# Layer 0's long-convolution filters moved ahead of the first conditioning block

## The chip, the cores and the metric

The kernel runs on one core of one Trainium2 chip, as one program. The metric is device time in microseconds (us) of one launch; lower is better. Three runs of the kernel before took 1815.71, 1817.62 and 1821.91 us, median 1817.62 us.

## The reference, cut to what matters

A two-layer network over 256 context and 256 latent tokens of 2048 features. In each layer a conditioning vector c is turned into a shift and a scale per feature by a matrix `ada_w` of 2048 x 6144; the normalised tokens, scaled and shifted, go through one wide projection `w_in` (2048 x 6688) whose columns feed four mixers. One of them (Hyena) convolves with filters of length 256 that a small network generates from the positions alone, so they depend on no token and no conditioning.

```python
for i in range(DEPTH):
    mod_l = jax.nn.silu(c) @ ada_w[i] + ada_b[i]
    mod_c = jax.nn.silu(c_ctx) @ ada_w[i] + ada_b[i]
    sh_l, sc_l, gt_l = jnp.split(mod_l[:, None, :], 3, axis=-1)
    ...
    h_l = _rmsnorm(x_l, norm_w[i]) * (1.0 + sc_l) + sh_l
    h_c = _rmsnorm(x_c, norm_w[i]) * (1.0 + sc_c) + sh_c
    pl = _project(h_l, w_in[i], SEG_NAMES)
    ...
    hy_l = _hyena_seq(pl['hy_x'], hy_conv_w[i], hy_conv_b[i], hy_filt, hy_bias[i])

def _hyena_filters(L, w1, b1, f1, w2, b2, f2, w3, b3, f3, w4):
    ...
    h = jnp.sin(f1 * (z @ w1 + b1))
    h = jnp.sin(f2 * (h @ w2 + b2))
    h = jnp.sin(f3 * (h @ w3 + b3))
    h = (h @ w4).reshape(L, 2, HY_ORDER, BR)
    ...
    return k * lax.rsqrt(jnp.sum(k * k, axis=0, keepdims=True) + EPS)
```

## The kernel before

Everything is float32. A weight w is split on the chip into two parts, `whi` (a cast on ScalarE, line 922) and `wlo` (w minus `whi`, on VectorE or GpSimd, line 180); the tokens likewise (tile `hs`). A projection is then three TensorE products per block: whi times high part, whi times low part, wlo times high part.

`run` (line 1407) starts a launch: it loads the 512 tokens in 16 tiles (line 1419), sums squares, makes `rrow` (one over the rms along the tokens, two lines from `junk` tiles, and a copy to a tile `mA`), and transposes the tokens into `xT`. Then `layer0_qk` computes the first eight projection units of 256 columns. It goes over the 2048 features in five stages, because a feature block can be projected only when its conditioning is known: `STAGES = (0, 1, 2, 4, 6, 8)`, so stages 0 and 1 hold 256 features each and stages 2 to 4 hold 512 each. For every stage:

- `ada` loads the stage's columns of `ada_w` in blocks of 256 KB through SyncE's queue into `raw` tiles (line 1037) and multiplies them on TensorE (psum tile `pa`, line 195): 16 loads for stage 0, 16 for stage 1, 32 for each later one. After the last block the sums are copied on ScalarE (`adr`), transposed on TensorE (`pa<-c_kc,adr`), and added to the bias (`mod`).
- `make_h` scales and shifts the feature blocks: `tr` on VectorE, `hs` high on ScalarE (line 1199), `hs` low on VectorE. It needs `mod` and `rrow`.
- every unit loads its 256 KB of `w_in` (line 934) and makes 12 products of 512 columns into psum tiles `pj` and `pB`. `steps` takes loads of the next stage's `ada` in between.

768 such products make up `layer0_qk`; stages 0 and 1 hold 96 each. The S5 mixer of layer 0 starts when they are done.

`hy_kf(0, ...)` (line 480) generates the filters. It is a Python generator, so nothing of it is issued until it is advanced. Its first part issues seven loads on SyncE's queue (four of `hy_w4`, line 486; two of `hydec`, line 489; one of `kdft`, line 491) and calls `hy_filters`: small loads on GpSimd's queue, one transposition to `hyv`, and three layers, each a TensorE product into psum tile `pA`, seven short VectorE instructions and a sine on ScalarE (line 476). The second part makes, for each of two orders, nine products of 128x512 into `pA` with VectorE multiplications, squares on ScalarE, additions on GpSimd, and four stores to DRAM (`kfd`, lines 531 and 532) on SyncE's queue. In `run` the whole generator was advanced inside `between(1)`, after stage 1's `make_h`; it is followed there by `s5_params(0)`.

The instructions' order on each engine isn't the order of the code. A scheduler simulates the program with its own costs, starts from the code's order as priority, takes what is ready, and allots buffers: two psum banks `pA`, two `pB`, three `pj`, nine `raw` tiles, 18 tiles each of `mA` and `mB`. The order that it writes is fixed: on the chip each engine goes through its own list in that order, and so does each queue of loads.

Of the kernel before, what the change touches and what calls it, by code (L numbers as in the profile page):

```python
# [15 lines left out]
PSUM = bass.MemoryType.PSUM  # L16
DRAM = bass.MemoryType.DRAM
# [5 lines left out]
T = 512  # L23
# [92 lines left out]
class Net:  # L116
# [36 lines left out]
    def const2(self, ap):  # L153
        """a constant of 512 columns or fewer, loaded where it is used"""
        t = self.t2()
        n = 1
        for d in ap.shape[1:]:
            n *= d
        v = t[:ap.shape[0], :n]
        if len(ap.shape) > 2:  # L160
            ap = ap.rearrange("p a b -> p (a b)")
        self.nc.scalar.dma_start(v, ap)
        return v
# [46 lines left out]
    def exp_acc(self, out, x, n, r, ni):  # L210
        """exp to float32 accuracy on small tiles: 2^n * poly(x - n ln 2); ni: int32 scratch"""
        nc = self.nc
        nc.vector.tensor_scalar(out, x, -104.0, 89.0, op0=OP.max, op1=OP.min)
        x = out
        nc.vector.tensor_scalar(n, x, 1.0 / math.log(2.0), MAGIC, op0=OP.mult, op1=OP.add)
        nc.vector.tensor_scalar(n, n, MAGIC, -127.0, op0=OP.subtract, op1=OP.max)
        nc.vector.tensor_scalar(n, n, 128.0, None, op0=OP.min)
        self.stt(r, n, -L1, x)
        self.stt(r, n, -L2, r)
        nc.vector.tensor_scalar(out, r, 1.0 / 5040, None, op0=OP.mult)  # L220
        for k in (720, 120, 24, 6, 2, 1):
            self.stt(out, out, 1.0 / k, r, op0=OP.add, op1=OP.mult)
        nc.vector.tensor_scalar(n, n, 127.0, None, op0=OP.add)
        self.cp(ni, n, 'v')
        nc.vector.tensor_scalar(ni, ni, 23, None, op0=OP.logical_shift_left)
        self.stt(out, out, 1.0, ni.bitcast(F32), op0=OP.add, op1=OP.mult)

    def rsqrt_mean(self, r, ss, n, c0=0, g=1):
        """r = 1/sqrt(ss/n + eps) on a small tile, on columns c0.. of each of g groups"""
        r, ss = (x.rearrange("p (g c) -> p g c", g=g)[:, :, c0:] for x in (r, ss))  # L230
        self.nc.scalar.activation(r, ss, AF.Sqrt, bias=self.eps[:r.shape[0]], scale=1.0 / n)
        self.nc.vector.reciprocal(r, r)

# [20 lines left out]
    def gla(self, i, v, qd, kd_, vd, lrs, lat_only, y_cb):  # L254
        """qd (x 1/8), kd_: [256, 512] and vd: [512 tok, 512] in DRAM; lrs: 4 tiles [128 tok, 32]"""
# [12 lines left out]
        t = self.t2()  # L268
# [5 lines left out]
        for ct in range(2):  # L274
# [9 lines left out]
            for d in range(2):  # L284
# [18 lines left out]
                kd = self.t2()  # L303
# [79 lines left out]
    def norm_out(self, o, r, lo, h, y_cb):  # L383
        """o: token tiles [128 tok, 128] of one head, r: their 1/rms -> y [128 dv, tokens]"""
        p = self.pm()
        for n, x in enumerate(o):
            self.nc.vector.tensor_scalar(x, x, r[:, n:n + 1], None, op0=OP.mult)
            self.tr(p[:, lo + n * 128:lo + (n + 1) * 128], x)
        y_cb(h, p)

# [1 line left out]
    def ret(self, qd, kd, vd, lat_only, y_cb):  # L392
        """qd, kd: [512, 512] and vd: [512 tok, 512] in DRAM"""
# [55 lines left out]
    def hy_filters(self, i):  # L449
        """the last hidden layer of the filter network, [64, 256 positions], twice on the partitions"""  # L450
# [28 lines left out]
    def hy_kf(self, i, kfd):  # L479
        """KF[order][parity][re/im] as tiles [128 m, 512 ch]; yields once its inputs are under way and after each order"""  # L480
# [54 lines left out]
    def hy_conv(self, v, ct, p, lat_only):  # L535
        """short conv of one tile of 128 channels from PSUM"""
# [11 lines left out]
    def hyena(self, i, v, kfd, xd, lat_only, y_cb):  # L548
        """xd: [1536, segs x 256] in DRAM"""
# [72 lines left out]
    def cmul(self, orr, oi, ar, ai, br, bi, t1, t2, eng=('v', 'v')):  # L622
        """(orr, oi) = (ar + i ai)(br + i bi)"""
# [8 lines left out]
    def s5_params(self, i):  # L632
        """per-layer arrays, (direction, state) on partitions and groups on the free axis"""
# [101 lines left out]
    def s5_gen(self, i, P, hb):  # L735
        """matrices of groups 4hb..4hb+3"""
# [71 lines left out]
    def s5_run(self, u, G, lat_only, y):  # L808
        """u: [(t, i), 4 groups x 64 chunks] -> y [(t, o), 4 groups x chunks]"""
# [50 lines left out]
    def s5_store_u(self, ud):  # L860
        """[128 ch, 512 tok] -> DRAM [group, (i, 7 - t), chunk], token = 8 chunk + t"""
# [69 lines left out]
    def wpart(self, src, r0, c0, w, step=True, keep=False):  # L931
        """rows r0..r0+255, columns c0..c0+w-1 of a weight matrix as hi and lo, [128, 2, w]; keep: in tiles of their own"""
# [21 lines left out]
    def proj_part(self, W, kq, c0, ps, t0, first, last, step=True):  # L954
        """rows 256 kq.. of (h @ W[:, c0:c0+256])^T into the two banks ps"""
# [10 lines left out]
    def proj_t(self, W, c0, ncol, t0, cb, step=True):  # L966
        """(h @ W[:, c0:c0+ncol])^T for tokens t0.., in tiles of 128 columns: cb(j, psum[:, tokens])"""
# [8 lines left out]
    def proj_n(self, W, c0, w, toks, cb, banks=None, order=range(8), step=True, keep=False):  # L976
        """x @ W[:, c0:c0+w] with tokens on partitions: cb(tt, psum[:, :w]); keep: one token tile after the other"""
# [44 lines left out]
    def ada(self, i, cols, n, group, done):  # L1022
        """n columns of the modulation from each of the two in cols, as four pieces of n / 2: row 32j + v of the
        result is piece j of stream v (0 latent, 1 context). Yields after every load; the products come after every
        group-th, as a change between them and full-width ones costs the tensor engine a drain."""
# [26 lines left out]
    def ada_cols(self, r, adab, k0, m):  # L1052
        """m[128, (sh, sc), k, v] for feature blocks k0.. from the four pieces (sh, sc) x 2 in r"""
# [10 lines left out]
    def ada_feat(self, i, f0, n, m, adab, group=GRP):  # L1064
        """the modulation of features f0..f0+n-1"""
        return self.ada(i, (f0, 2048 + f0), n, group, lambda r: self.ada_cols(r, adab, f0 // 128, m))

    def ada_el(self, i, cols, nv, done, eng):
        """ada for 512 columns from each of the two in cols and the first nv streams, with the products off the
        tensor engine, which only sums over the partitions"""  # L1070
# [66 lines left out]
    def gate_row(self, i, v, j):  # L1137
        """512 columns of the gate of stream v on every partition"""
# [22 lines left out]
    def rstd(self, ss):  # L1161
        """ss [128, token tiles, pieces] -> 1/rms [128, token tiles]"""
# [7 lines left out]
    def rrow(self, rs):  # L1170
        """[128, 512]: 1/rms of the 4 x 128 tokens along the columns, on every partition"""
# [9 lines left out]
    def warm_sqrt(self, ss):  # L1181
        """brings the square root's table in before it is waited for"""
# [3 lines left out]
    def make_h(self, k, x, m, vec, rrow):  # L1186
        """hi and lo of block k of h^T from x^T [128, 512]; rrow: 1/rms along the tokens"""
# [52 lines left out]
    def qk_units(self, lat):  # L1240
        """the projections of s5_u and of the q and k of GLA and retention: (name, width, first token, callback)"""
# [7 lines left out]
    def layer0_qk(self, xT, m, adab, vec, rrow, between):  # L1249
        """the projections of qk_units in layer 0, over the feature quarters as their modulation becomes known"""  # L1250
# [141 lines left out]
    def w_out(self, i, c, toks, t0, x, gt, ss, step=True, done=None):  # L1392
        """column piece c (256 wide) of x += gate * (y @ w_out); sums of squares of the rows"""
# [13 lines left out]
    def run(self, out):  # L1407
# [15 lines left out]
        hk = self.hy_kf(0, kfd[0])  # L1423
        ss = self.sm.tile([128, 4, 8], F32, name="xss")
# [13 lines left out]
        self.hh, self.hl = [], []  # L1438
        Ps = {}

        def between(f):
            self.cur = 'A'
            if f == 1:
                for _ in hk:
                    pass
# [140 lines left out]
```

## Time and profile before

| | us |
|---|---|
| median of three runs (lowest to highest) | 1817.62 (1815.71 to 1821.91) |
| profiled execution: span from first to last instruction | 1809.3 |
| TensorE busy | 1714.9 (95%) |
| VectorE busy | 1283.9 (71%) |
| ScalarE busy | 753.5 (42%) |
| GpSimd busy | 552.2 (31%) |

The profile gives the span of the profiled execution and no other time of it; the median run is 8.3 us longer than that span (launch and end lie outside it), and this distance is taken as it is. PE is TensorE's matmuls and PEld its weight loads; DVE, ACT, POOL and SP are VectorE, ScalarE, GpSimd and SyncE, and a name with q is the engine's issuing side, where loads are issued. One matmul of float32 data by this program shows as several records, and neighbouring records overlap by about a tenth of a us, since their ends are modelled. A load is listed where it is issued, with the time that the issue took.

### The profile page before, as it was taken

What the parts mean: (1) busy time and instruction counts of PE and PEld (TensorE: products, weight loads), DVE (VectorE), ACT (ScalarE), POOL (GpSimd) and SP (SyncE); (2) the same over time, 40 slices, a digit from 0 to 9 for tenths busy, and PEclk for the clock granted to TensorE, in tenths of its full rate; (3) what the DMA queues carried; (4) which work ended last, traced back from release to release, by engine and by line L of the source; (5) the groups of instructions that cost most, each with busy time, mean ns of one, the idle gap of its engine ahead of it and who ended that gap; (6) DMA issues with size and microseconds to landing.
All of it is one profiled execution on the core that took longest, in us unless ns stands there. A gap on an engine that the chain in (4) does not pass through costs nothing. (4 is left out here: it accounts for less than half of the span.)

```text
span 1809.3 us, 33542 instructions
## 1 busy us (share of the span) xinstructions
PE 1714.9 (95%) x12320; PEld 1412.7 (78%) x12320; DVE 1283.9 (71%) x2393; ACT 753.5 (42%) x1462; POOL 552.2 (31%) x524
## 2 busy tenths in 40 slices
PE   7999999998999999999999999698999899999997
PEld 4656678877766668876788899477987788999997
DVE  2477774669997666965888584777768776668754
ACT  5333252244344434232334434555354545454544
POOL 4024022223323100101144734468434231121353
PEclk9999999999999999999999999799999999999999
DMA  9868755556464678668866555466453336788963
GB/s 295 258 233 234 248 169 165 167 172 202 126 182 152 194 220 266 197 204 267 290 213 213 173 154 182 121 184 205 140 164 108 105 91 196 239 262 256 283 202 123
DMA packets 308029, 355.18 MB, mean 196 GB/s; under 512 B 42433, under 2 KB 227481, under 8 KB 307865
## 3 DMA queue, kind: packets, MB, share of 16 engines
q1 hardware_dynamic: 299936, 341.81, 61.1%
q10 hardware_dynamic: 5112, 8.79, 1.6%
q0 software_dynamic: 2816, 2.43, 0.9%
q8 instruction: 97, 1.59, 0.4%
q14 instruction: 68, 0.55, 0.1%
HBM read 316.11 MB, written 36.83 MB: 195 GB/s over the span
## 5 line engine op out<-in xcount | busy, mean ns | idle before, releaser
L195 PE MATMUL pj<-hs,whi 128*128 128x512 f32 (+1 forms) x2560 | 692.2, 356 | 12.8 <-ACT hs L1199 6.9
L922 ACT CAST whi<-raw 128x512 fp32r<-128x512 f32 (+1 forms) x536 | 329.6, 619 | 608.8 <-DMA raw<-in_w_in_dram 271.9
L180 DVE TENSOR_TENSOR wlo<-raw,whi 128x512 fp32r<-128x512 f32 (+1 forms) x428 | 334.1, 786 | 275.1 <-ACT whi L922 263.7
L195 PEld LDWEIGHTS pj<-hs,whi 128*128 128x128 f32 x2560 | 443.3, 190 | 104.2 <-issue 27.4
L994 PE MATMUL pj<-whi,hs 128*128 128x256 f32 (+1 forms) x2368 | 455.0, 289 | 5.8 <-ACT tr L1377 2.3
L195 PE MATMUL pj<-hs,wlo 128*128 128x512 f32 (+1 forms) x1280 | 451.2, 354 | 1.1 <-DVE wlo L180 1.0
L180 POOL TENSOR_TENSOR wlo<-raw,whi 128x512 fp32r<-128x512 f32 (+1 forms) x108 | 159.4, 1476 | 793.5 <-ACT whi L922 680.6
L994 PEld LDWEIGHTS pj<-whi,hs 128*128 128x128 f32 x2368 | 374.0, 191 | 24.0 <-issue 15.4
L994 PE MATMUL pj<-wlo,hs 128*128 128x256 f32 (+1 forms) x1184 | 340.8, 288 | 0.0
L195 PEld LDWEIGHTS pj<-hs,wlo 128*128 128x128 f32 x1280 | 241.9, 189 | 38.6 <-issue 6.5
L180 POOL TENSOR_TENSOR mA<-mA 128x512 f32<-128x512 f32 x120 | 173.9, 1462 | 226.5 <-ACT mA L511 84.7
L994 PEld LDWEIGHTS pj<-wlo,hs 128*128 128x128 f32 x1184 | 226.0, 191 | 4.3 <-issue 3.8
L195 PE MATMUL pA<-mA 128*64 128x64 f32 (+6 forms) x1276 | 160.6, 307 | 25.9 <-DVE mA L180 19.5
L180 DVE TENSOR_TENSOR mA<-mA 128x512 f32<-128x512 f32 (+6 forms) x246 | 155.0, 658 | 22.3 <-DMA mA<-rq 17.8
L192 DVE SCALAR_TENSOR_TENSOR acc<-raw,sc,acc 128x512 f32<-128x512 f32 x180 | 142.1, 819 | 8.4 <-DMA raw<-in_ada_w_dram 8.2
L195 PEld LDWEIGHTS pA<-mA 128*64 128x64 f32 (+3 forms) x1276 | 102.8, 151 | 57.6 <-issue 16.7
L195 PE MATMUL pB<-mB 64*64 64x128 f32 (+4 forms) x896 | 101.8, 293 | 6.7 <-DVE mB L180 4.3
L180 POOL TENSOR_TENSOR acc<-acc,raw 128x512 f32<-128x512 f32 x60 | 88.6, 1477 | 63.1 <-ACT raw L1086 52.6
L180 DVE TENSOR_TENSOR mB<-mB 128x512 f32<-128x512 f32 (+2 forms) x164 | 84.1, 546 | 14.1 <-ACT mB L292 8.3
L195 PEld LDWEIGHTS pB<-mB 64*64 64x64 f32 (+2 forms) x896 | 66.0, 152 | 30.1 <-issue 13.5
L173 ACT COPY mA<-pA 128x512 f32<-128x512 f32 (+3 forms) x118 | 45.2, 409 | 97.0 <-PE pA L195 70.0
L195 PE MATMUL pa<-raw,sc 128*32 128x256 f32 (+1 forms) x1024 | 79.7, 360 | 3.5 <-DMA raw<-in_ada_w_dram 2.3
(230 smaller groups left out, 1779.7 us busy)
## 6 DMA issues: line engine op xcount, KB each, us to landing
raw<-in_ada_w_dram SPq DMA_DIRECT2D x384, 256.0 KB, 3.9
raw<-in_w_in_dram SPq DMA_DIRECT2D x384, 256.0 KB, 3.4
raw<-in_w_out_dram SPq DMA_DIRECT2D x128, 256.0 KB, 3.3
raw<-in_w_in_dram SPq DMA_DIRECT2D x32, 272.0 KB, 3.1
mB<-kfd SPq DMA_DIRECT2D x24, 256.0 KB, 4.3
mB<-in_ctx_dram SPq DMA_DIRECT2D x16, 256.0 KB, 5.6
mB<-in_x_dram SPq DMA_DIRECT2D x16, 256.0 KB, 5.9
kfd<-mA SPq DMA_DIRECT2D x16, 256.0 KB, 4.3
```

The costliest lines, as they stand in the source:

```text
L173: self.nc.scalar.copy(out, in_)
L180: (self.nc.vector if eng == 'v' else self.nc.gpsimd).tensor_tensor(out, a, b, op=op)
L192: self.nc.vector.scalar_tensor_tensor(out, in0, scalar, in1, op0=op0, op1=op1)
L195: self.nc.tensor.matmul(out, lhsT, rhs, start=start, stop=stop)
L922: self.nc.scalar.copy(hi, x)
L994: mm = lambda a, b, start, stop: self.nc.tensor.matmul(o, a, b, start=start, stop=stop, skip_group_check=per > 1)
```

## The change

The generator is advanced once right after it is made, ahead of the sums of squares and of `rrow`, so that the seven loads and the filter network come there in the code; the rest of it runs after the token transpositions and ahead of `layer0_qk`. `between(1)` no longer advances it.

```diff
         hk = self.hy_kf(0, kfd[0])
+        next(hk)
         ss = self.sm.tile([128, 4, 8], F32, name="xss")
...
         self.hh, self.hl = [], []
+        self.cur = 'A'
+        for _ in hk:
+            pass
         Ps = {}
 
         def between(f):
             self.cur = 'A'
-            if f == 1:
-                for _ in hk:
-                    pass
             if f == 1:
                 Ps[0] = self.s5_params(0)
```

The other lines of the diff remove comments. What the scheduler made of it is seen in three places.

**SyncE's queue of loads, from the last token tiles on.** `in_x` and `in_ctx` are the tokens, `in_ada_w` the conditioning's blocks (256 KB each), `in_w_in` the projection's weights. Before:

```order
L1419 DMA mB<-in_x_dram 128x512 x2
L1037 DMA raw<-in_ada_w_dram 128x2x256 x16
L934 DMA raw<-in_w_in_dram 128x2x256
L486 DMA mA<-in_hy_w_dram 64x512
L1037 DMA raw<-in_ada_w_dram 128x2x256 x3
L934 DMA raw<-in_w_in_dram 128x2x256
L486 DMA mA<-in_hy_w_dram 64x512
L1037 DMA raw<-in_ada_w_dram 128x2x256 x2
```

With the change:

```order
L1419 DMA mB<-in_x_dram 128x512 x2
L486 DMA mA<-in_hy_w_dram 64x512 x4
L489 DMA mA<-const_hydec_dram 128x512 x2
L491 DMA mA<-const_kdft_dram 128x512
L1037 DMA raw<-in_ada_w_dram 128x2x256 x16
L934 DMA raw<-in_w_in_dram 128x2x256
L1037 DMA raw<-in_ada_w_dram 128x2x256 x3
L934 DMA raw<-in_w_in_dram 128x2x256
L1037 DMA raw<-in_ada_w_dram 128x2x256 x3
```

The filters' seven loads now stand ahead of stage 0's 16 blocks. After those 16, stage 1's 16 blocks stand in the next 22 loads, with six of `w_in` between.

**TensorE, around the first projection product (`pj<-hs,whi`).** `pa<-raw,sc` are the conditioning's products, four for each block; `pA<-mA` here the filter network's layers; `pA<-junk` the products of `rrow`; `pa<-c_kc,adr` the transposition that ends a stage's conditioning. Before:

```order
L195 MATMUL pA<-junk,c_kc 128x128
L195 MATMUL pa<-raw,sc 32x128 x36
L199 MATMUL pa<-c_kc,adr 128x128
L195 MATMUL pa<-raw,sc 32x128 x12
L195 MATMUL pj<-hs,whi 128x512 x3
```

With the change (the row ahead of these is the transposition that ends stage 0):

```order
L195 MATMUL pA<-mA 64x256
L195 MATMUL pa<-raw,sc 32x128 x24
L195 MATMUL pA<-mA 64x256
L195 MATMUL pa<-raw,sc 32x128 x24
L195 MATMUL pA<-mA 128x256
L195 MATMUL pA<-junk,c_kc 128x128 x2
L195 MATMUL pa<-raw,sc 32x128 x8
L195 MATMUL pA<-junk,c_kc 128x128
L195 MATMUL pa<-raw,sc 32x128 x4
L195 MATMUL pA<-junk,c_kc 128x128
L195 MATMUL pa<-raw,sc 32x128 x4
L199 MATMUL pa<-c_kc,adr 128x128
```

The first product of the projections, which stood behind three blocks of stage 1, now follows this list: behind the three filter layers, the four products of `rrow` and all 64 products (16 blocks) of stage 1. After five projection products come the first eight products of stage 2, which need four of its blocks. The 18 products of 128x512 that make the filters still stand between projection products, now between the 19th and the 172nd instead of the 172nd and the 321st.

**ScalarE, up to the first scaled tokens (`hs<-tr,mod`, line 1199).** `adr<-pa` ends a stage's conditioning, L476 is the filter network's sine, `mA<-pA` the copy of `rrow`. Before:

```order
L173 COPY mA<-pA 128x512
L173 COPY adr<-pa 128x128
L922 CAST whi<-raw 128x2x256
L1199 ACTIVATE hs<-tr,mod_146 128x256 x4
L922 CAST whi<-raw 128x2x256
```

With the change:

```order
L476 ACTIVATE mA<-mA 64x256
L922 CAST whi<-raw 128x2x256 x2
L476 ACTIVATE mA<-mA 64x256
L922 CAST whi<-raw 128x2x256 x2
L173 COPY mA<-pA 128x512
L476 ACTIVATE mA<-mA 128x256
L173 COPY adr<-pa 128x128
L1199 ACTIVATE hs<-tr,mod_146 128x256 x8
```

The scaled tokens of stages 0 and 1 now come together, behind the third sine and behind the copy that ends stage 1's conditioning.

## Rows read from the trace of the kernel before

**Rows 1.** Busy time in stretches: opening projections, and the S5 and GLA start.

```profile
core 0: us, PE busy (x) PEld busy (x) DVE busy (x) ACT busy (x) POOL busy (x), PEclk, DMA share, GB/s
...
36.69:108.00 71.31, 70.41 (x444) 45.00 (x442) 37.21 (x78) 25.22 (x47) 1.29 (x1) 0.99 0.85 270
...
340.00:420.00 80.00, 69.22 (x672) 60.14 (x671) 58.13 (x92) 28.87 (x55) 24.23 (x28) 0.94 0.58 174
```

**Rows 2.** TensorE's waits from 36 to 300 us: total, times, longest.

```profile
PE pj L195 <- ACT hs L1199: 1.4, 1, 1.4
PE pa L195 <- PE pa L199: 1.0, 1, 1.0
```

**Rows 3.** TensorE's timeline: start, duration, count; projection products in stage 0.

```profile
54.31 0.62 PE L195 MATMUL pj<-hs,whi 128*128 128x512 f32 x2
54.76 0.40 PE L195 MATMUL pj<-hs,wlo 128*128 128x512 f32 x1
55.00 0.63 PE L195 MATMUL pj<-hs,whi 128*128 128x512 f32 x2
```

**Rows 4.** SyncE's timeline: the issue of stage 0's blocks.

```profile
13.60 14.07 SPq L1037 DMA_DIRECT2D raw<-in_ada_w_dram  x16
```

**Rows 5.** Loads, 0 to 62 us: GB/s in 40 slices; issues with KB each.

```profile
GB/s 0 174 163 224 313 374 378 365 335 330 329 366 336 346 350 339 323 309 290 282 214 330 297 270 252 272 271 346 362 347 333 274 172 272 303 287 314 329 89 319
...
mA<-in_hy_w_dram SPq DMA_DIRECT2D x4, 128.0 KB, 6.0
mA<-const_hydec_dram SPq DMA_DIRECT2D x2, 256.0 KB, 6.5
mA<-const_kdft_dram SPq DMA_DIRECT2D x1, 256.0 KB
```

**Rows 6.** TensorE's timeline: end of stage 0's conditioning, first projection products.

```profile
31.22 0.63 PE L195 MATMUL pa<-raw,sc 128*32 128x128 f32 x8 [0.30 <-DMA raw<-in_ada_w_dram]
...
36.69 1.65 PE L195 MATMUL pj<-hs,whi 128*128 128x512 f32 x3
38.13 0.63 PE L195 MATMUL pj<-hs,wlo 128*128 128x512 f32 x1
```

**Rows 7.** ScalarE's and VectorE's timelines: the steps ahead of scaled tokens.

```profile
64.83 0.62 ACT L922 CAST whi<-raw 128x512 fp32r<-128x512 f32 x1 [3.36 <-DMA raw<-in_w_in_dram]
...
93.63 0.42 ACT L476 ACTIVATE mA<-mA 128x256 f32<-128x256 f32 x1 [1.94 <-PE pa L195]
...
61.17 0.29 ACT L173 COPY adr<-pa 128x128 f32<-128x128 f32 x1
...
67.62 1.70 ACT L1199 ACTIVATE hs<-tr,mod 128x256 fp32r<-128x256 f32 x4
...
65.48 0.69 DVE L180 TENSOR_TENSOR wlo<-raw,whi 128x512 fp32r<-128x512 f32 x1 [4.43 <-ACT whi L922]
...
81.79 0.86 DVE L192 SCALAR_TENSOR_TENSOR mA<-mA 64x256 f32<-64x256 f32 x2
82.68 0.29 DVE L208 TENSOR_SCALAR mA<-mA 64x256 f32<-64x256 f32 x1
```

**Rows 8.** Conditioning's tile `pa` alone, as busy time, from 36.69 to 61 us.

```profile
36.69:61.00 24.31, 5.58 (x106) 3.36 (x104) 0.00 (x0) 0.00 (x0) 0.96 0.94 282
```

**Rows 9.** TensorE's timeline: first and third layer of the filter network.

```profile
67.03 0.64 PE L195 MATMUL pA<-mA 33*64 33x256 f32 x2
...
86.95 0.70 PE L195 MATMUL pA<-mA 64*128 64x256 f32 x2
```

**Rows 10.** Stretches of 1 us; the last column but two is TensorE's granted clock.

```profile
36.00:37.00 1.00, 1.00 (x9) 0.59 (x6) 0.85 (x3) 0.19 (x1) 0.00 (x0) 0.50 1.04 258
...
39.00:40.00 1.00, 1.00 (x6) 0.79 (x6) 0.00 (x0) 0.00 (x0) 0.00 (x0) 1.00 1.04 271
```

**Rows 11.** SyncE's queue from 36 to 200 us: waits in total, times, longest.

```profile
SPq L531 <- POOL mA L180: 6.6, 3, 5.2
```

**Rows 12.** TensorE's waits from 300 to 420 us.

```profile
PE pA L195 <- DVE mA L180: 5.0, 1, 5.0
```

## The prediction

> **What bounds the kernel now.** I read the busy time by stretches first, then TensorE's waits, then the opening us by us. From 36.69 to 108 us TensorE is busy 70.41 of 71.31 us [rows 1], and from 36 to 300 us its two largest waits are 1.4 and 1.0 us, each once [rows 2]. The reader should see that from 36.69 us, where the first projection product starts [rows 6], TensorE has work without a break for some 250 us. Products of 512 columns follow each other at 0.23 us: three from 54.31 to 55.00 us [rows 3]. Ahead of 36.69 us it waits for loads: stage 0's last block arrives for the products at 31.22 us [rows 6]. Whatever delays the first projection product, and isn't paid back by work that TensorE did meanwhile, therefore delays everything behind it.
>
> **The seven loads.** Four of 128 KB and three of 256 KB [rows 5] are as much as five of the conditioning's blocks of 128 x 512 numbers, which are as large as one of the latter three. Sixteen blocks are issued in 14.07 us [rows 4], 0.88 us each, the pace at which the loads flow. They now stand ahead of stage 0's blocks, so the products that began at 31.22 us begin 5 x 0.88 = 4.4 us later, at 35.6 us. Before, they were spread behind stage 0, among blocks that TensorE didn't yet need.
>
> A page of the Trainium skill, "DMA: Bandwidth & Descriptors" (section "Where 436 GB/s comes from"), gives about 358 GB/s as what HBM allows one core; by that, an estimate, a block would take 0.73 us and the sum below would be 4 us less. The blocks of rows 4 went at 0.88 us, and the sum goes by them.
>
> **The wait for stage 1.** This is the large term. In the new order TensorE makes all of stage 1's products ahead of the first projection product. Stage 1's last block is the 22nd load behind stage 0's: 22 x 0.88 = 19.4 us, so it lands at about 55.0 us. The filter network runs meanwhile; its three layers wait for blocks in the same list, so they cost nothing but the tail. The tail: the sixth `w_in` load lands one place earlier, 54.1 us; its cast takes 0.62 us, its subtraction 0.69, and behind it on VectorE stand an instruction of 0.43 and a clipping of 0.29 [rows 7]; that is 56.1 us. Then ScalarE does the sine (0.42), the copy of stage 1's sums (0.29) and the first two scaled halves (two of the four in 1.70 us, 0.85) [rows 7]: 57.6 us. So the first projection product starts 57.6 - 36.69 = 20.9 us later.
>
> The tail isn't in the trace of before in this form. From below it is the copy and the two halves alone, 1.1 us; from above the 5.5 us that passed before from 31.22 to 36.69 us [rows 6]. I take 2.6, since each of its instructions has a row.
>
> **What is paid back.** Stage 1's products no longer interrupt the projections: 5.6 us of `pa` work lay behind 36.69 us [rows 8]. The three layers of the filter network, 0.64 us for the first and the second and 0.70 for the third [rows 9], are also done; they overlap their neighbours a little, so about 1.9. With what overlaps, 7.5 us are paid back. `hyv`'s transposition and the like are within the rounding.
>
> **What is new behind the start.** After five projection products TensorE needs four blocks of stage 2, seven loads behind stage 1's last: 55.0 + 6.2 = 61.2 us. The clock is at its lower level then, 1.2 of 2.4 GHz, as it was at 36 to 37 us (0.50) after a thin stretch, and back at 39 us [rows 10]; the first three products took 1.44 us, 0.48 each [rows 6]. So the five end at about 60.0 us and TensorE waits 1.2 us. The lower level costs about what it cost before, plus the time that this wait keeps it low: another 1.2 us, an estimate from those 0.48 against 0.23 us. From below both are nothing, if the loads are quicker.
>
> **What costs nothing.** The 18 products of 128x512 remain among the projection products, only earlier, and TensorE pays them in either place. VectorE's multiplications and GpSimd's additions stay beside TensorE's work: VectorE is busy 37.21 of 71.31 us there [rows 1]. If that cover were gone, their psum banks would hold TensorE up. The ScalarE sines move into its idle opening. The four first stores of filters now stand on SyncE's queue amid stage 2's blocks; before, a store held that queue for up to 5.2 us [rows 11]. Nine `raw` tiles in hand and `w_in` tiles already split cover that; uncovered it is 5.2 us more. Taking the filters off stage 2's end may spare the two waits of rows 2: 2.4 us less at most. From some 940 projection products on, the order on TensorE is that of before; the S5 mixer's first instructions stand where they stood, and a late start reaches them whole.
>
> **The sum.** 20.9 - 7.5 + 1.2 + 1.2 = 15.8 us. Against the profiled execution: 1809.3 + 15.8 = 1825.1 us of span, and with the 8.3 us by which the median lies above that span, 1833.4 us; I say 1833.4.
>
> **Bounds of this case.** Below: all 27 loads at the highest rate of the opening, 378 GB/s [rows 5], 0.69 us a block, 5.1 us less; a tail of 1.1, 1.5 less; no wait and no added low clock, 2.4 less; the waits of rows 2 gone, 2.4 less: +4.4 us, 1822. Above: a tail of 5.5, 2.9 more; a store that holds the queue, 5.2 more: +23.9 us, 1841.5. An effect of over 0.3% (5.5 us) is what a measurement of this kernel can tell from no change.
>
> **Rivals.**
>
> *TensorE catches up.* If the projections aren't limited by TensorE itself, a late start lets blocks and weights pile up, and the products then run closer together until the 15.8 us are made up: 1817.6 us. For it: weight loads fill only 45.00 of 71.31 us, 63% [rows 1], which would leave 26 us. Against it: the matmuls fill that stretch, and the products of rows 3 stand 0.23 us apart with no wait between them while the next ones are ready; nothing in these rows shows them closer. A page of the Trainium skill, "Perfetto Trace Analysis" (section "Identifying the Most-Contended Engine"), says that matmul busy time is no good measure of how near TensorE is to its limit and that weight-load share is one; by that rule this rival would be the likeliest. The trace has no matmuls at a closer spacing to support it. Chance 0.06.
>
> *The S5 start absorbs it.* From 340 to 420 us TensorE is busy 69.22 of 80 us [rows 1], and its longest wait there is 5.0 us for VectorE [rows 12]. The change brings S5's parameters forward, from behind the 373rd projection product to behind the 192nd, so if these 10.8 us come of S5's VectorE work being late, they go: with the waits of rows 2, 15.8 - 10.8 - 2.4 = +2.6 us, 1820, not slower than a measurement can tell. It decides if VectorE reaches that point with no backlog. Against it: the second S5 group's products stand behind the same projection product as before. Chance 0.09.
>
> *Only the loads count.* The change doesn't do what it says, since the filters' products stay amid the projections; if in fact stage 1's blocks don't hold the first product up, only the 4.4 us of loads remain: 1822. The order speaks against it. Chance 0.05.
>
> *SyncE's queue clogs.* The four early stores, each as long as the longest before (5.2 us), hold stage 2's blocks for 21 us, and `raw` tiles cover only part: about 12 us more, 1845. For it: the stores stand between blocks that TensorE needs soon. Against it: the filters' products stand well ahead. Chance 0.08.
>
> **How the numbers follow.** The forecast has 0.72, at 1833.4, with its own range 1822 to 1841. The range 1821 to 1841 holds most of it, the third rival and part of the second; what it leaves out is the first rival, the last, and the edges, under 2 in 10. Slower by over 0.3%: 0.72 less its lowest edge (0.02), and 0.08 and a share of the second and third, 0.83. Within 0.3%: the rest of these and the first, 0.13. Faster: an overshoot of the first two, 0.04.
>
> **What would show it.** In the profile after: the first `pj` product at 55 to 60 us instead of 36.69; `pa` products of stage 1 all ahead of it; the last products of `layer0_qk`, and the S5 mixer's first ones after them, about 15 us later than before, and every later landmark by as much. TensorE's products still 0.23 us apart. If the first product comes before 45 us, the wait for stage 1 is wrong; if it comes late but the end doesn't, TensorE had room to catch up; if the delay grows beyond 20 us after 60 us, the queue or the stores are the cause.

## Result and the profile after

The changed kernel takes 1851.42 us (median of four runs, 1845.74 to 1854.04), the kernel before beside it 1819.76 us. The ratio is 1.0173, with a 95% interval of 1.0149 to 1.0196: 31.7 us slower, twice the 15.8 us forecast and outside the range of 1821 to 1841 us. The direction was right, the size wrong.

Nothing was added to or taken from the computation. TensorE is busy 1735.4 us, 20 more than before, though it does the same work; stretches at a lower granted clock, as the one below, can be a part of it.

```profile
PE 1735.4 (94%) x12320; PEld 1426.5 (77%) x12320; DVE 1285.2 (70%) x2393; ACT 754.9 (41%) x1462; POOL 541.8 (29%) x524
```

**The start came as forecast.** ScalarE's timeline in the changed kernel shows the step that the prediction worked out: cast, copy of `rrow`, third sine, `adr`, first scaled tokens.

```profile
53.43 0.62 ACT L922 CAST whi<-raw 128x512 fp32r<-128x512 f32 x1 [2.38 <-DMA raw<-in_w_in_dram]
54.01 0.59 ACT L173 COPY mA<-pA 128x512 f32<-128x512 f32 x1
55.53 0.42 ACT L476 ACTIVATE mA<-mA 128x256 f32<-128x256 f32 x1 [0.93 <-DVE mA L208]
55.85 0.25 ACT L173 COPY adr<-pa 128x128 f32<-128x128 f32 x1
56.00 1.71 ACT L1199 ACTIVATE hs<-tr,mod 128x256 fp32r<-128x256 f32 x4
```

And TensorE's timeline, the first projection product at 56.95 us (57.6 forecast, 36.69 before in [rows 6]):

```profile
56.95 0.87 PE L195 MATMUL pj<-hs,whi 128*128 128x512 f32 x2 [0.48 <-ACT hs L1199]
```

**What came besides.** TensorE's waits from 36 to 300 us, which were 1.4 and 1.0 us in [rows 2]:

```profile
PE pa L195 <- DMA raw<-in_ada_w_dram: 12.6, 7, 7.3
PE pa L199 <- ACT adr L173: 1.5, 2, 1.3
```

TensorE's timeline shows where: two waits for conditioning blocks at the start of stage 3's conditioning, and products 0.42 us apart behind them, where [rows 3] had 0.23.

```profile
142.35 0.76 PE L195 MATMUL pa<-raw,sc 128*32 128x256 f32 x4 [2.17 <-DMA raw<-in_ada_w_dram]
150.45 1.07 PE L195 MATMUL pa<-raw,sc 128*32 128x256 f32 x4 [7.34 <-DMA raw<-in_ada_w_dram]
...
153.75 0.63 PE L195 MATMUL pj<-hs,whi 128*128 128x512 f32 x1
154.17 0.63 PE L195 MATMUL pB<-hs,whi 128*128 128x512 f32 x1
```

The stretches have the columns of [rows 1]. From 144 to 156 us TensorE is busy 5.55 of 12 us, at a granted clock of 0.50. And from 60 to 110 us it is busy all the time while the loads run at 145 and 99 GB/s, where [rows 1] had 270. From 110 to 140 us they run at 266 GB/s again.

```profile
60.00:80.00 20.00, 20.00 (x94) 12.58 (x87) 9.62 (x17) 11.67 (x23) 3.87 (x3) 0.98 0.46 145
80.00:110.00 30.00, 30.00 (x122) 19.48 (x125) 14.43 (x18) 8.69 (x15) 12.25 (x15) 1.00 0.31 99
...
144.00:156.00 12.00, 5.55 (x15) 3.78 (x16) 3.28 (x14) 2.27 (x4) 0.00 (x0) 0.50 0.98 271
```

Just ahead of the waits, GpSimd issues eight loads of S5's parameters. They belong to `s5_params(0)`, which follows the filters in `between(1)`. Its timeline in the changed kernel, first and last of their rows:

```profile
135.15 2.18 POOL L702 DMA_DIRECT2D mA<-in_s_b_re_dram  x2
...
141.74 0.75 POOL L725 DMA_DIRECT2D mA<-in_s_c_im_dram  x1
```

In the kernel before, the first of them was issued at 168.01 us:

```profile
168.01 2.18 POOL L702 DMA_DIRECT2D mA<-in_s_b_re_dram  x2
```

**How far the delay goes.** Right behind the 768 products of `layer0_qk` stands one row that every kernel has, the first product of GLA's v. TensorE's timeline, before:

```profile
286.90 0.39 PE L994 MATMUL pj<-whi,hs 128*128 128x272 f32 x1
```

and after:

```profile
316.02 0.39 PE L994 MATMUL pj<-whi,hs 128*128 128x272 f32 x1
```

So 29.1 us are lost up to there. A second profile of each kernel (last rounds below) has this row at 286.82 and 315.36 us: 28.5 us. The first profile of before is of a quick execution (1809.3 us of span, 1813.8 in the second). What follows takes 1522 and 1527 us in the two profiles of before, 1532 and 1525 in those of after: executions of one program scatter there. These profiles show no more than a few us that the change could add; the medians put it at 3 us (31.7 less 28.8). The question is thus the 13 us above the forecast, ahead of that row.

### The profile page after: what moved, and what is told of

The parts are those of the page before. It is cut to its first block, busy times and chain, and to the rows that moved or that the text cites. A ratio compares the mean times of both kernels' runs of the same rounds, so it can differ in the third digit from the quotient of the medians.

```text
span 1847.6 us, 33550 instructions
## 1 busy us (share of the span) xinstructions
PE 1735.4 (94%) x12320; PEld 1426.5 (77%) x12320; DVE 1285.2 (70%) x2393; ACT 754.9 (41%) x1462; POOL 541.8 (29%) x524
## 5 line engine op out<-in xcount | busy, mean ns | idle before, releaser
L994 PEld LDWEIGHTS pj<-whi,hs 128*128 128x128 f32 x2368 | 374.5, 191 | 22.4 <-issue 15.7
L180 POOL TENSOR_TENSOR mA<-mA 128x512 f32<-128x512 f32 x120 | 165.9, 1395 | 213.1 <-DVE hs L192 65.1
L192 DVE SCALAR_TENSOR_TENSOR acc<-raw,sc,acc 128x512 f32<-128x512 f32 x180 | 146.1, 842 | 8.9 <-DMA raw<-in_ada_w_dram 8.9
L195 PE MATMUL pa<-raw,sc 128*32 128x256 f32 (+1 forms) x1024 | 89.5, 376 | 16.1 <-DMA raw<-in_ada_w_dram 13.9
```

The source lines that it names most:

```text
L180: (self.nc.vector if eng == 'v' else self.nc.gpsimd).tensor_tensor(out, a, b, op=op)
L192: self.nc.vector.scalar_tensor_tensor(out, in0, scalar, in1, op0=op0, op1=op1)
L195: self.nc.tensor.matmul(out, lhsT, rhs, start=start, stop=stop)
L994: mm = lambda a, b, start, stop: self.nc.tensor.matmul(o, a, b, start=start, stop=stop, skip_group_check=per > 1)
```

## Experiments

Three theories. A: the eight loads of S5's parameters take the transfers from blocks that TensorE needs at once. B: the filters' stores (`kfd`) hold SyncE's queue, and blocks stand behind them. C: blocks are late because their `raw` tiles come free late. The late start is common to all. The rows of the table are named by their edits, which the rounds below explain; `rrow` stands for the filters' first part moved behind `rrow`.

| kernel | first projection product, us | first product of GLA's v, us | median us | ratio to before, 95% interval |
|---|---|---|---|---|
| before (two profiles) | 36.69, 36.30 | 286.90, 286.82 | 1817 to 1820 | |
| changed (two profiles) | 56.95, 57.35 | 316.02, 315.36 | 1851.4 | 1.0173 (1.0149 to 1.0196) |
| parameters one stage later | 57.65 | 315.49 | 1850.2 | 1.0182 (1.0151 to 1.0213) |
| stores from GpSimd | 57.90 | 310.30 | 1842.4 | 1.0142 (1.0112 to 1.0172) |
| first part behind `rrow` | 38.45 | 303.22 | 1836.2 | 1.0103 (1.0069 to 1.0138) |
| `rrow`, parameters later | 37.70 | 302.87 | 1835.2 | 1.0101 (1.0075 to 1.0127) |
| `rrow`, stores | 39.38 | 306.42 | 1832.6 | 1.0080 (1.0049 to 1.0112) |
| stores, parameters later | 56.35 | 308.59 | 1842.2 | 1.0135 (1.0108 to 1.0162) |
| all three | 39.70 | 303.60 | 1831.8 | 1.0074 (1.0047 to 1.0101) |
| before, seven loads early | 41.90 | 301.58 | 1835.1 | 1.0090 (1.0060 to 1.0119) |
| changed, no S5 loads | 57.31 | 303.50 | 1840.0 | 1.0126 (1.0096 to 1.0156) |
| `rrow`, stores, no S5 loads | 39.20 | 293.14 | 1824.4 | 1.0040 (1.0025 to 1.0055) |
| before, no S5 loads | 36.58 | 286.50 | 1816.5 | 0.9993 (0.9972 to 1.0014) |
| changed, S5 loads at stage 3 | 57.28 | 308.88 | 1843.7 | 1.0137 (1.0113 to 1.0161) |
| same, stores from GpSimd | 58.27 | 308.46 | 1838.0 | 1.0112 (1.0094 to 1.0130) |
| `rrow`, stores, S5 loads at stage 3 | 39.20 | 297.02 | 1829.8 | 1.0069 (1.0049 to 1.0089) |

The two middle columns are one profiled execution each; the pairs of profiles agree within 0.7 us. Scatter can be larger: "`rrow`, stores" and "all three" have the same order on TensorE and on SyncE's queue and are 2.8 us apart at GLA's v, "stores from GpSimd" and "stores, parameters later" 1.7.

### First round: late start, stores, S5's parameters

S5's parameters one stage later:

```diff
-            if f == 1:
+            if f == 2:
                 Ps[0] = self.s5_params(0)
```

> The changed kernel, with S5's parameters generated one stage later (behind stage 2's scaled tokens instead of stage 1's); the filters stay ahead of the first conditioning block, so the late start (first projection product at 57 us) stays. Theory A (the late start costs about 16 us, and S5's parameter loads, issued at 135 to 142 us amid conditioning blocks that TensorE needs next, cost the other 12 or so): TensorE's two waits for blocks of 2.2 and 7.3 us near 142 and 150 us go, and the low clock after them; the time falls from about 1851 to 1838 us, ratio to the kernel before 1.010. Theory B (the filters' stores hold SyncE's queue, and blocks come late for that): the stores stay, so the waits stay, 1851 us, ratio 1.017.

1850.2 us, no change. This is not an answer on theory A: the edit left the loads where they were. The scheduler put them at the same place, as GpSimd's timeline of this kernel shows:

```profile
134.31 2.18 POOL L702 DMA_DIRECT2D mA<-in_s_b_re_dram  x2
```

The filters' stores from GpSimd's queue (in `hy_kf`, layer 0 alone):

```diff
-                nc.sync.dma_start(kfd[o, 0, ri], y)
-                nc.sync.dma_start(kfd[o, 1, ri], x[0])
+                q = nc.gpsimd if i == 0 else nc.sync
+                q.dma_start(kfd[o, 0, ri], y)
+                q.dma_start(kfd[o, 1, ri], x[0])
```

> The changed kernel, with the eight stores of layer 0's filters issued from GpSimd's queue instead of SyncE's, so that no block of the conditioning stands behind a store. Theory A (S5's parameter loads collide with the blocks): the waits of 2.2 and 7.3 us near 142 and 150 us stay within 2 us, 1851 us, ratio to the kernel before 1.017. Theory B (stores hold SyncE's queue; in the changed kernel it waits 8.1 us for GpSimd's additions ahead of stores between 58 and 160 us): those waits go, 8 to 13 us less, 1838 to 1843 us, ratio 1.010 to 1.013.

1842.4 us, 5.7 us earlier at GLA's v. The two long waits became several short ones (the longest 1.4 us), and the clock stayed higher. The time is inside theory B's range, but TensorE still waits for blocks 6.7 us in nine pieces, and 23.4 us at GLA's v remain. Theory B explains a part at most.

The generator's first part behind `rrow`, so that `rrow` no longer stands behind the filter network:

```diff
         hk = self.hy_kf(0, kfd[0])
-        next(hk)
...
         rrow = self.rrow(self.rstd(ss[:, :, :4]))
+        next(hk)
```

> The changed kernel, with the generator's first part (seven loads, filter network) advanced behind rrow instead of ahead of it; everything else stays, the filters still come ahead of the first projections in the code. The scheduler then puts the first projection product behind one block of stage 1, not behind all sixteen. Theory A (the wait for stage 1's blocks makes the late start): the first product comes at 37 to 42 us instead of 57. If the start's 20 us are worth 16 at the end, and the collision of S5's loads stays, 1832 to 1836 us, ratio 1.007 to 1.009; if the collision only hurts when TensorE has no blocks in hand, about 1820 to 1825, ratio 1.000 to 1.003. Rival (the start isn't what counts): 1845 or more, ratio above 1.014.

The first product comes at 38.45 us and the time is 1836.2 us: the late start is worth 12.8 us at GLA's v (316.02 less 303.22), if nothing else changed with it (S5's loads now come at 148.41 us). But 16.3 us against the kernel before remain, with an early start. Something else of that size is in the change.

> Both edits of the two runs on the start and on S5's parameters together: the generator's first part behind rrow, and S5's parameters one stage later. Theory A: neither the late start nor the collision is left; 1820 to 1825 us, ratio 1.000 to 1.003, and no wait of TensorE above 3 us between 60 and 200 us. Rival (something else of the change costs the missing 12 us, the filters' own work ahead of the projections, say): 1830 us or more.

1835.2 us. As the parameters' edit moves nothing, this repeats the run above.

### Second round: the edits combined, the loads alone

> The kernel with the filters' first part behind rrow (1836 us measured) and, besides, the eight stores of layer 0's filters issued from GpSimd's queue. In that run TensorE waited 2.1 and 3.7 us near 160 and 164 us, for a block and for a projection weight, after SyncE's queue had stood behind three stores from 138.5 to 148.6 us. Theory B' (the stores hold the queue, and with it what TensorE needs next): those waits and the low clock behind them go, 6 to 10 us less, 1826 to 1830 us, ratio to the kernel before 1.004 to 1.007. Theory A (S5's parameter loads of 148 to 156 us slow the blocks): 1834 to 1838, ratio 1.009 to 1.011.

1832.6 us, above the 1826 to 1830 of theory B'. The waits of the run before it, 2.14 and 3.70 us, grew to 3.95 and 4.43. TensorE's timeline:

```profile
164.41 0.94 PE L195 MATMUL pa<-raw,sc 128*32 128x256 f32 x4 [3.95 <-DMA raw<-in_ada_w_dram]
169.79 2.07 PE L195 MATMUL pj<-hs,whi 128*128 128x512 f32 x4 [4.43 <-ACT whi L923]
```

SyncE's queue now stands still without any store, for a `raw` tile that TensorE releases late (waits of 120 to 175 us; line 935 is the `w_in` load, 934 before):

```profile
SPq L935 <- PE pa L195: 12.1, 2, 11.0
```

and when it goes on at 150 us it meets S5's loads (151 to 158 us). The stretch then has a full DMA share at 112 GB/s, and TensorE runs dry:

```profile
160.00:165.00 5.00, 1.05 (x8) 0.14 (x4) 0.47 (x2) 0.00 (x0) 0.00 (x0) 0.96 1.07 112
```

So theory B falls as the main cause: a queue held for other reasons does the same. A and C are left.

> The changed kernel with both edits that leave the start alone: the filters' stores from GpSimd's queue (1842 us alone) and S5's parameters one stage later (1850 us alone). If the stores hid the collision (a queue held by stores has fewer blocks under way that S5's loads could slow), the second edit now shows: 1834 to 1838 us, ratio 1.009 to 1.011. If S5's loads cost nothing here in either case: 1842 us, ratio 1.013 to 1.015.

> All three edits: first part of the filters behind rrow, stores from GpSimd's queue, S5's parameters one stage later. What then is left of the change is the seven loads ahead of stage 0's blocks and the filters' products ahead of stage 2. If late start, stores and collision are all there is: 1818 to 1824 us, ratio 0.999 to 1.003. If the filters' products in stages 0 and 1 cost something of their own: 1828 or more.

1842.2 and 1831.8 us, as the same kernels without the parameters' edit (1842.4, 1832.6), for the reason above.

The seven loads alone, early, in the kernel before:

```diff
     def hy_kf(self, i, kfd):
...
+        if i == 0:
+            yield
         h = self.hy_filters(i)
...
         hk = self.hy_kf(0, kfd[0])
+        next(hk)
```

> The kernel before, with only the seven loads (hy_w4, hydec, kdft) issued ahead of stage 0's blocks; the filter network and everything else stay where they were. By the term of the prediction (16 blocks in 14.07 us, five blocks' worth of loads): first projection product 4.4 us later, at 41 us, and 4.4 us at the end, 1823 us, ratio 1.002. The run with the first part behind rrow has the same seven loads there and its first product at 38.5 us only: by that 1.8 us, 1820, ratio 1.001.

1835.1 us: a clear miss. The first product is 5.2 us late, as the term of the loads says, but 14.7 us are lost at GLA's v. The stretches show the rest near 200 us, behind S5's loads, which this kernel issues at 189 to 196 us:

```profile
195.00:200.00 5.00, 5.00 (x34) 3.39 (x33) 2.58 (x16) 0.00 (x0) 1.33 (x2) 1.00 1.03 136
200.00:205.00 5.00, 2.56 (x20) 0.82 (x18) 0.00 (x0) 0.00 (x0) 0.00 (x0) 1.00 1.04 289
205.00:210.00 5.00, 3.18 (x8) 2.49 (x9) 3.06 (x13) 1.24 (x2) 0.00 (x0) 0.66 0.60 205
```

The filters' products weren't moved here. Only S5's loads met the blocks at another moment. By the records of TensorE, the 431st projection product is 7.5 us later than in the kernel before and the 441st 14.0. That pointed back to theory A; in this kernel it was not tried by taking the loads out.

### Third round: without S5's loads

In `s5_params` of layer 0, the tiles of b and c are set to zero on GpSimd, and the eight loads are left out:

```diff
+            if i == 0:
+                nc.gpsimd.memset(x, 0.0)
-            for r_ in range(2):
+            for r_ in range(2) if i else ():
                 nc.gpsimd.dma_start(x[r_ * 64:(r_ + 1) * 64].rearrange("p (g i) -> p g i", i=16),
```

and the same for the loads of c.

> The changed kernel without the eight loads of layer 0's in_s_b_re, in_s_b_im, in_s_c_re and in_s_c_im on GpSimd's queue: their tiles are set to zero instead, so S5's b and c of layer 0 are left out of the computation. All other work stays and TensorE's and SyncE's order is that of the changed kernel (the edit of one stage later had left these loads at 134 to 141 us, so it did not test them). Theory A (these loads take the queues from the conditioning's blocks): the waits of 2.2 and 7.3 us near 142 and 150 us shrink below 2 us, the clock stays up, 10 to 14 us less than the changed kernel: 1837 to 1841 us, ratio to the kernel before 1.010 to 1.013. Theory C (blocks are late because their raw tiles come free late): 1848 to 1852, ratio 1.016 to 1.018.

> The kernel with the filters' first part behind rrow and the stores from GpSimd's queue (1833 us), without the same eight loads of layer 0 (S5's b and c set to zero). There TensorE waited 3.95 us for a block at 164 us and 4.43 us for a projection weight at 170 us, while the loads moved at 112 to 171 GB/s. Theory A: both waits and the low clock behind them go, 10 to 12 us less: 1820 to 1823, ratio 1.000 to 1.003. Theory C: 1830 to 1834, ratio 1.006 to 1.009.

> The kernel before without the same eight loads of layer 0 (S5's b and c set to zero): the control. There the loads moved at 161 GB/s from 175 to 180 us, and TensorE waited for nothing, as it had blocks and weights in hand. Both theories: same as before within 3 us, ratio 0.998 to 1.000. If it is 5 us faster or more, typical runs of the kernel before lose time to these loads too, and its quick profile hides it.

Theory A holds in all three. The changed kernel falls to 1840.0 us and reaches GLA's v 12.5 us earlier, the one with an early start to 1824.4 us (1 us above theory A's range) and 13.3 us earlier (10.5 against "all three", which with the loads has the same order), and the kernel before stays where it was. TensorE's waits from 36 to 300 us in the changed kernel without the loads, and the stretch that had a clock of 0.50:

```profile
PE pa L195 <- DMA raw<-in_ada_w_dram: 5.6, 7, 1.6
```

```profile
144.00:156.00 12.00, 12.00 (x56) 8.65 (x55) 8.81 (x39) 1.86 (x3) 0.00 (x0) 1.00 0.64 211
```

The two waits are still there, but short:

```profile
139.57 0.62 PE L195 MATMUL pa<-raw,sc 128*32 128x256 f32 x4 [0.48 <-DMA raw<-in_ada_w_dram]
141.82 0.62 PE L195 MATMUL pa<-raw,sc 128*32 128x256 f32 x4 [1.62 <-DMA raw<-in_ada_w_dram]
```

TensorE's order is that of the changed kernel only up to some 185 us (175 without the loads); behind that the scheduler ordered anew. Most of the gain lies ahead of that: the projection product at 138.99 us in the changed kernel, ahead of the waits, comes at 137.90 here, 1.1 us earlier, and the one at 157.79 us, behind them, at 146.46, 11.3 us earlier.

Theory C falls as a cause by itself. In the kernel with an early start and without the loads, SyncE's queue stands as long for a `raw` tile as with them (waits of 120 to 175 us; line 938 is the `w_in` load there):

```profile
SPq L938 <- PE pa L195: 13.8, 4, 11.0
```

And yet TensorE is busy 15.00 of 15 us from 155 to 170 us, while the loads run at 321 to 339 GB/s.

The transfers of 134 to 151 us show why the loads matter. First the changed kernel: q1 is the queue of SyncE, q0 that of GpSimd, with packets, MB and the share of 16 engines; the third row has KB and us to landing.

```profile
q1 hardware_dynamic: 1812, 2.76, 60.2%
q0 software_dynamic: 480, 1.08, 37.7%
...
raw<-in_ada_w_dram SPq DMA_DIRECT2D x8, 256.0 KB, 11.0
```

Without the eight loads:

```profile
q1 hardware_dynamic: 3168, 4.82, 83.3%
q0 software_dynamic: 96, 0.03, 0.8%
...
raw<-in_ada_w_dram SPq DMA_DIRECT2D x11, 256.0 KB, 4.1
```

In the same 17 us, 1.05 MB of S5's parameters came in and 2.06 MB less of blocks and weights (4.82 less 2.76), and a block took 11.0 us to land, in the median, instead of 4.1.

Why the kernel before loses nothing: while its eight loads move, at 161 GB/s, TensorE has products in hand and is busy throughout.

```profile
175.00:180.00 5.00, 5.00 (x22) 2.89 (x20) 4.89 (x18) 0.00 (x0) 0.34 (x1) 1.00 0.96 161
```

> The kernel before once more, for a second profile: its first span was 1809.3 us and seven more runs of it gave a median of 1818 to 1820. If that first profile was a quick execution, this one's span is 1814 to 1821 us, and the difference shows where runs of the same program differ; if time lies around the span, the span is near 1810 again.

Its span is 1813.8 us and its time 1815.67 us: 1.9 us lie around the span.

### Fourth round: S5's loads held until stage 3

All computed again; each tile that the loads fill is first written from a scaled token of stage 3:

```diff
-            if f == 1:
-                Ps[0] = self.s5_params(0)
+            if f == 3:
+                Ps[0] = self.s5_params(0, self.hl[-1].bitcast(F32)[:, 0:1])
...
+            if late is not None:
+                nc.gpsimd.tensor_scalar(x[:, 0:1], late, 0.0, None, op0=OP.mult)
```

> The changed kernel, all of it computed, with S5's parameters of layer 0 called at stage 3, and each of the tiles that the eight loads of S5's b and c fill first written (one column, on GpSimd) from a scaled token of stage 3, so that the loads cannot be issued before about 200 us. Theory A (they cost what they cost because TensorE needs the blocks behind them at once): like the changed kernel without these loads, 1837 to 1842 us, ratio to the kernel before 1.010 to 1.014, if TensorE has blocks in hand at stage 3 as it had in the kernel before; if they hit TensorE there too, 1848 or more.

> The same with the filters' stores from GpSimd's queue. If the stores cost time only together with S5's loads, as in the changed kernel without these loads (768 products done 15.7 us later than before, with the stores on SyncE's queue): the same as the run beside it within 3 us, 1836 to 1842. If the stores cost on their own: 6 to 9 us less, 1830 to 1835, ratio 1.007 to 1.010. What is left is the late start, which the prediction put at 15.8 us: 1833.

> The kernel with the filters' first part behind rrow and the stores from GpSimd's queue (1833 us), with S5's loads held until stage 3 in the same way. Neither late start nor collision is left: 1820 to 1825, ratio 1.001 to 1.004. If it were below 1814 us it would beat the kernel before; nothing seen so far would bring that.

GpSimd's timeline of the first of these, and TensorE's longest wait for blocks in it, show that the loads moved this time and the collision at 140 us went:

```profile
199.25 2.25 POOL L704 DMA_DIRECT2D mA<-in_s_b_re_dram  x2
```

```profile
142.63 0.63 PE L195 MATMUL pa<-raw,sc 128*32 128x256 f32 x4 [1.93 <-DMA raw<-in_ada_w_dram]
```

It takes 1843.7 us, 2 us above its range, with 7.1 us at GLA's v won of the 12.5 that leaving the loads out won: at 200 us they cost less, not nothing. Moving the stores as well changes GLA's v by 0.4 us (308.88 to 308.46), against 5.7 with S5's loads beside them: up to there the stores cost time together with those loads, hardly by themselves. (Without S5's loads the delay is 16.6 us at GLA's v and at the 768th product, not the 15.7 of the expectation.) The median, 1838.0 against 1843.7 us, says 5.7 us, most of it behind that row, where executions scatter; whether the stores cost anything there stays open. The third kernel, 1829.8 us, missed its 1820 to 1825 and beats nothing. No version tried is faster than the kernel before.

> The changed kernel once more, for a second profile: whether the 768th projection product is again 29 us later than before (302 to 319 us), with the same two waits of TensorE near 142 and 150 us, and how much of the other 8 or 9 us behind it, in layer 1, comes back. If those are scatter of single executions, they vary by 3 us or more; if they come of the order, they stay within 1 us.

The row of GLA's v is at 315.36 us, the wait at 150 us is there again with 5.97 us, and the span is 1840.2 us, 26.4 above the second span of before. (By TensorE's records the 768th product stands at 284.69 us before and at 313.81 and 313.15 us in the two profiles of the changed kernel.)

## Why the prediction was wrong

**Up to GLA's v the sum came near for what it counted, in part by luck.** Without S5's eight loads, the changed kernel reaches GLA's v 16.6 us later than before (303.50 less 286.90); the sum said 15.8. By the medians that kernel is 22.8 us slower (1840.01 less 1817.17; interval 17.4 to 28.3). The steps one by one:

- The seven loads: 4.4 us; alone in the kernel before, they delay the first product by 5.2 us.
- The wait for stage 1: 57.6 us; measured 56.95 and 57.35.
- What is paid back, 7.5 us: not seen by itself. Without S5's loads the start's 20.6 us ended as 16.6, a net 4.0 where the sum had 5.1 (7.5 less 1.2 less 1.2). In these 4.0 are waits for blocks of 5.6 us that the sum did not have, so two sizes were off against each other.
- The wait behind five products, 1.2 us, did not come: TensorE is busy 23.05 of 23.05 us from 56.95 to 80 us. The lower clock did: it was 0.50 from 58 to 60 us and 1.00 at 61 us.
- Nothing behind the S5 mixer but the late start, as TensorE's order is that of before from some 940 products on: not so in layer 1. TensorE's order differs again from 1168 to 1296 us (times of before). Near 1250 us both profiles of the changed kernel have a wait for ScalarE of 5.21 and 5.03 us, where those of before have 0.37 and none at these products, and near 1065 us one for GpSimd of 3.67 and 4.18, where those of before have 1.39 and 1.01. The medians leave 3 us for all of this; what of it the change causes was not tried.

**The step that failed is "What costs nothing".** It weighed the filters' products, sines and stores, and left out what follows the generator in `between(1)`. With the generator gone from there, `s5_params(0)` comes 33 us earlier, from 168.01 to 135.15 us, though the whole program has become later. Its eight loads then meet the blocks of stage 3's conditioning, and TensorE's list asks for these at once. The waits there are 2.17 and 7.34 us, against 0.48 and 1.62 without the loads: 7.4 us. The lower clock (5.55 us of busy time at half speed) adds 2.8 us, an estimate: 10.2 in all. The gain of the kernel without the loads grows by as much between the products on either side of the waits (from 1.1 to 11.3 us), and is 12.5 at GLA's v. The prediction did see that S5's parameters come forward, but in a rival, and only as a possible gain for VectorE. Every instruction of a moved step counts, its DMAs too; so do those of the step behind it.

Blocks had no lead to lose, for a second reason that the prediction touched and priced at nothing: "nine `raw` tiles in hand and `w_in` tiles already split cover that". The tiles were full, but of weights that were split late and of blocks that TensorE's list uses late. SyncE's queue waited for both from 60 to 110 us, when the loads ran at 99 to 145 GB/s. Its two largest waits there, in the changed kernel:

```profile
SPq L1037 <- DVE wlo L180: 16.7, 4, 6.6
SPq L1037 <- PE pa L195: 12.4, 4, 7.2
```

Without S5's loads the same two waits of the queue are 16.7 and 12.9 us, the loads run at 144 and 99 GB/s, and TensorE's longest wait for a block is 1.6 us. So a small lead did no great harm by itself; that these tiles set it was not tried apart.

A page of the Trainium skill, "DMA: Bandwidth & Descriptors" (section "Issuing engines are not separate DMA queues"), says that transfers issued by different engines run on the same 16 DMA engines and interleave. The trace agrees: q0 had 37.7% of the 16 engines while SyncE's blocks took 11.0 us to land instead of 4.1. The same page of the Trainium skill (section "Why small descriptors are slow (HBM only)") speaks of a fixed overhead for each packet and for each DMA operation. In the trace, 1.08 MB in 37.7% of 17 us is 168 GB/s, and 4.82 MB in 83.3% is 340 GB/s. But q0's packets aren't the smaller ones (1.08 MB in 480, 4.82 MB in 3168), and the profile doesn't list the pieces within a packet, so no run here shows what makes that difference.

**The rivals.** TensorE did not catch up: of the start's 20.6 us, 16.6 were left at GLA's v without S5's loads, and the products stayed 0.23 us apart. S5's start absorbed 1 us at most: the delay is 29.1 us at GLA's v and, by TensorE's records, 28.4 us at 449 us (time of before). "Only the loads" was wrong in its price: the loads alone cost 15 us in all, some 6.5 of it behind S5's loads near 200 us; that these are the cause there is argued, not tried. "SyncE's queue clogs" came nearest in time (1845), and its stores count in part at most: moving them won 5.7 us at GLA's v while S5's loads were there and 0.4 when they were held back. The last of the prediction's signs, a delay beyond 20 us after 60 us, came and pointed to the queue or the stores; loads on another queue were not among its suspects.

The 8.3 us that the prediction put around the span were wrong too: 1.8 us lie there (1849.39 us of time, 1847.6 of span). The forecast is hardly touched, as its difference was added to the median.

**What is left.** With an early start, stores from GpSimd and no S5 loads, 6.2 us remain at GLA's v (293.14 less 286.90), 2.5 of them at the first product. What makes the rest wasn't tried.

## What to carry to other kernels

When a step is moved in a program that a scheduler orders, list what stood behind it and now comes earlier, with its DMAs, and look up what is in flight at the new moment: here eight loads that nobody edited cost 10 to 12 of the 29 us. An engine that is busy all the time can still live from hand to mouth; a low rate of transfers in the stretch ahead is a reason to ask whether it has a lead, though it did little harm here without the eight loads. And an edit that is to move a load must be seen to have moved it, in that engine's timeline, before its time says anything.

## What the hardware showed that was not expected

Eight loads of 128 KB, 1.05 MB in all, left 2.06 MB less of others within 17 us, and a block's landing took 11.0 us instead of 4.1 (medians). After a stretch in which TensorE had mostly waited (0.94 us busy from 140 to 144 us), its granted clock was 0.50, the lower of 1.2 and 2.4 GHz, from 144 to 156 us; in the kernel without these loads it was 1.00 there. And two executions of one program differ by 5 to 7 us behind GLA's v, but by 0.1 to 0.7 us up to it (by 0.4 to 2.8 us in kernels that share the order of TensorE and SyncE).
